# A two-layer mLSTM/retention trunk: longer waits between the steps of the gate chain, and a second buffer for head outputs

## The chip, the cores and the metric

The kernel runs on one core of one Trainium2 chip. The metric is the device time of one execution in microseconds (us); less is better. Five engines of the core take part. TensorE (PE) does matrix products and has a second sequence of weight loads (PEld) beside it, VectorE (DVE) and ScalarE (ACT) do elementwise work, GpSimd (POOL) does elementwise work and issues some DMAs, and SyncE (SP) issues most DMAs. Each engine runs its own list of instructions in a fixed order and waits at an instruction until the semaphores that it needs have been raised.

## The reference

The input is x with 1024 positions of 1024 features; there are two layers and a final RMSNorm. Each layer computes

```
h = RMSNorm(x) * (1 + scale) + shift
p = h @ W_in                                   # one wide projection
y_m = mLSTM, 4 heads of 256                    # q, k (after a short causal convolution), v, i, f, o, z
y_r = retention, 4 heads of 256                # q, k (after rotary), v, z
x = x + gate * (concat(y_m, y_r) @ W_out)
```

The mLSTM heads have two scalar gates for each position. The input gate i enters as exp(i), the forget gate f as a log-sigmoid, and both are summed along the positions under a running maximum:

```
b     = cumsum(log_sigmoid(f));  a = b + m
g     = b[l] - b[s] + i[s]                     # s <= l
m_row = max(a, max_s g)
h     = (exp(g - m_row) . (q k^T)) v / max(|den|, exp(-m_row))
```

A head's output is then normalised over its 256 features, with a LayerNorm or a GroupNorm, before it is multiplied by its gate path.

## The kernel before, in words

**Numbers.** Every operand of a large product is kept as a pair of a high and a low part, and a product of such pairs takes three matmuls (`mm3`, L177 to L179). A high part comes from an ACT cast (L404) and a low part from a subtraction on DVE or POOL (L409).

**Products.** The projection W_in is done by a scheme with 7 products instead of 8 for each block. It needs sums of the normalised input, the forms U1 to U4, which `build_forms` makes on DVE (L634 to L655). The jobs of the plan are named after what they project. A v job makes the values of two heads with 24 matmuls of 256 columns a product, about 2.9 us; the z, q, k and a jobs have 12 matmuls of 512 columns a product. The products of a job are called a11, S1, S2, a12, S3, S4 and a22. They gather in PSUM banks (px, pz) which other engines empty before the next product can write them. L775 is the ACT copy of such a bank for the q, k and z jobs, L778 and L785 are their DVE sums, L825, L826, L832 and L835 are the copy and the sums of the v jobs, and L843 is the Tanh of a z job. L832, the sum with S3, is the one after which the bank of S3 is free for a22.

**Order.** The order of PE is the order of the program, written by hand. For the other engines a scheduler orders the instructions by a simulated time line, except those marked `late` (and those of a `Later()` object, line L144 in the profile), which keep the order of the program. Side work is written as generators which are launched beside the products: after each product `tick()` runs those that are due, and `yield n` makes one wait n products.

**Gate chain.** `gate_chain` is such a generator, launched once in each layer after the two small products for the gate columns. It has 4 heads by 8 tiles of 128 positions, hence 32 rows of 128. Its steps are: ACT moves the two gate rows out of PSUM (L512); a DMA stores them (L515) and another loads them back as 32 rows (L531); ACT takes Abs, Exp and Ln (L533 to L535); DVE makes the log-sigmoid and two running sums; PE carries the sums over the tiles (L547); DVE adds the carry and makes a running maximum; PE turns the maxima of the tiles into one row (L556); DVE takes their running maximum; PE turns them back (L561); DVE adds, and a DMA stores the maxima (L567); PE transposes four arrays (L571), a DMA loads the maxima for all partitions (L575), and ACT makes three tables of exponentials (L580, L585, L596). The DVE steps go through `Later()`, so they keep their place in the program. The 32-row arrays lie in the two buffers of the pool tag "q", which the attention of the heads uses later.

**Around it.** In layer 0 the chain runs beside two more gate projections, the rotary tables (`rotary_tables`, also through `Later()`) and the v job of heads 4 and 5, then come the v job of heads 6 and 7 and the jobs z4, q4 and k4. In layer 1 it runs beside the two gate projections and the v job of heads 4 and 5, and z4 follows directly. The mLSTM heads, 0 to 3, come after the four retention heads in each layer.

**Head outputs.** `attention` is a generator for each head, and its step `values` gathers the output of a pair of tiles in a buffer: "nd" (516 columns, one buffer) for mLSTM heads, "n" (512 columns, one buffer) for retention heads. ACT writes it (L1134 for the inter-chunk part or L1148 in the first step of an mLSTM head, L1150 for retention), for mLSTM DVE adds the product (L1155), then DVE takes the statistics (L1163, L1164), ACT normalises in place (L1185), and a DVE transpose (L1192) into "zt" frees the buffer. `load_rotary` (L971) takes four 512-column buffers for the sine and cosine of the rotary step; one of them is of tag "nd". It does so at the job q4 and they are used until the rotary step of k7 is done.

Of the kernel before, what the change touches and what calls it, by code (L numbers as in the profile page):

```python
# [24 lines left out]
HD = 256  # L25
# [62 lines left out]
def tile_hybrid_trunk(ctx, tc, x, xt, c, positions, w_ada, b_ada, norm_g, w_in, w_blk, w_val, conv_w, conv_b,  # L88
# [16 lines left out]
    def nm(s):  # L105
        uid[0] += 1
        return f"{s}_{uid[0]}"

    def bt(dt=F32, n=512):
        return big.tile([P, n], dt, tag="b", name=nm("b"))  # L110

    def wt(tag, n, bufs, dt=F32):
        t = wrk.tile([P, 516 if tag == "acc" else n], dt, tag=tag, bufs=bufs, name=nm(tag))
        return t[:, 0:n] if tag == "acc" else t

    def ps_a():
        return pa.tile([P, 512], F32, tag="a", name=nm("pa"))
# [386 lines left out]
    def gate_chain(l, pgs, gt):  # L504
# [5 lines left out]
        for half in range(2):  # L510
            for r in (0, 32):
                A.activation(raw[r:r + 4, half * HALF:(half + 1) * HALF], pgs[half][r:r + 4, :], AF.Identity,  # L512
                             bias=bg[r:r + 4, :])
        for i in range(2):
            Q.dma_start(gtd[l][i], raw[32 * i:32 * i + 4, :])  # L515
        one, two = (wt("q", 1024, 2) for _ in range(2))
# [9 lines left out]
        nc.vector.memset(first, 1.0)  # L526
        nc.vector.memset(first.rearrange("p (h t) -> p h t", h=4)[:, :, 0:1], 0.0)
        nc.vector.memset(exc, 0.0)
        yield 3
        for i, t in enumerate((fb, li)):  # L530
            Q.dma_start(t, gtd[l][i].rearrange("h (b t) -> (h b) t", t=P))  # L531
        yield 3
        A.activation(e, fb, AF.Abs)  # L533
        A.activation(e, e, AF.Exp, scale=-1.0)
        A.activation(e, e, AF.Ln, bias=ones[0:32, 0:1])  # L535
        yield 2
        V.scalar_tensor_tensor(fb, fb, 0.0, e, ALU.min, ALU.subtract)
        V.tensor_scalar(lfq, fb, MAG_Q, -MAG_Q, ALU.add, ALU.add)
        V.tensor_tensor(fb, fb, lfq, ALU.subtract)
# [1 line left out]
        V.tensor_tensor_scan(br, on, fb, 0.0, ALU.mult, ALU.add)  # L541
        V.tensor_scalar(liq, li, MAG_Q, -MAG_Q, ALU.add, ALU.add)
        V.tensor_tensor(lir, li, liq, ALU.subtract)
        yield 3
        pc = ps_a()
        for i, b in enumerate((bq, br)):
            PE.matmul(pc[0:32, i:i + 1], lower, b[:, P - 1:P], start=True, stop=True)  # L547
# [3 lines left out]
        V.tensor_tensor(u, liq, bq, ALU.subtract)  # L551
        V.tensor_tensor_scan(mx, on, u, 0.0, ALU.mult, ALU.max)
        V.tensor_tensor(v, lir, br, ALU.subtract)
        yield 3
        pm = ps_a()
        PE.transpose(pm[0:1, 0:32], mx[:, P - 1:P], ident[0:32, 0:32])  # L556
        V.tensor_tensor_scan(inc[0:1], first[0:1], pm[0:1, 0:32], 0.0, ALU.mult, ALU.max)
        V.tensor_tensor(exc[0:1, 1:32], inc[0:1, 0:31], first[0:1, 1:32], ALU.mult)
        yield 3
        pb = ps_a()  # L560
        PE.matmul(pb[0:32, 0:1], exc[0:1, :], ones[0:1, 0:1], start=True, stop=True)  # L561
        V.tensor_copy(carry[:, 2:3], pb[0:32, 0:1])
# [408 lines left out]
    def load_rotary(rot):  # L971
        for which in range(2):
            for i in range(2):
                t = wt("dm", 512, 2) if which == 0 else wt("nd", 516, 1) if i == 0 else bt()
                Q.dma_start(t[:, 0:HALF], rdr[which][i])
                A.activation(t[:, 0:HALF], t[:, 0:HALF], AF.Sin, scale=2.0 * math.pi)
                rot[which].append(t[:, 0:HALF])
# [7 lines left out]
    def attention(l, hg, gt):  # L985
        h, ml = hg % 4, hg < 4
        W = HD + 2 if ml else HD
        sds = [None] * NCH
        nrm = [None] * NCH
        st = {"state": None, "cf": None}  # L990
# [115 lines left out]
        def values(j, tts):  # L1106
            state = st["state"]
            sH, sL = sds[j]
            if tts[0] == 0:
                st["nd"] = wt("nd", 516, 1).rearrange("p (a b) -> p a b", a=2) if ml else None  # L1110
                nrm[j] = st["nd"][:, :, 0:HD] if ml else wt("n", 512, 1).rearrange("p (a b) -> p a b", a=2)
            nd3 = st["nd"]
            ahead = {}
            if j == 0:
# [92 lines left out]
        def run(what):  # L1207
            op, a = what[0], [int(x) for x in what[1:]]
            j = a[0]
            if op in "qk":  # L1210
                load_qk(op, j)
            elif op in "QK":
                split_qk(op.lower(), j)
            elif op == "v":
                load_v(j)
            elif op == "t":
                kt_load(j)
            elif op == "s":
                kt_split(j)
            elif op == "d":  # L1220
                dm_load(j)
            elif op == "m":
                dm_make(j)
            elif op == "S":
                begin(scores(j))
            elif op == "V":
                values(j, tuple(a[1:]))
            elif op == "U":
                begin(update(tuple(a)))
# [240 lines left out]
    for l in range(DEPTH):  # L1470
# [23 lines left out]
        if l == 0:  # L1494
# [10 lines left out]
            for step in script.split():  # L1505
# [50 lines left out]
                elif what == "G":  # L1556
                    n = arg[0]
                    finish_gsh(0, 2 * n, 2, pad[:, 4 * n:4 * n + 2], pad[:, 4 * n + 2:4 * n + 4])
                elif what == "W":
                    i, p = arg  # L1560
                    wsp[i, p] = high(rw[i][p], q3[:, p * 512:(p + 1) * 512] if i == 2 else None)
                else:
                    i, p = arg
# [25 lines left out]
        launch(build_forms(hT, F))  # L1589
        run_units(gate_units(wg, hT, pgs))  # L1590
        launch(gate_chain(l, pgs, gt), 1)
        if l == 0:
            launch(rotary_tables(), 7)
# [26 lines left out]
        def job_product(what, arg):  # L1620
            h = arg[0]
            if what == "v":
                return vpair_product(l, F, arg)
            if what == "z":
                return pair_product(F, z_done(gdr[l][h]))
            if what == "a":
                return pair_product(F, zo_done(gdr[l][h][arg[1]]))
            which = int(what == "k")
            if h == 4 and not which:
                load_rotary(rot)  # L1630
            if h > 3:
                return pair_product(F, rot_done(l, h, which, *rot), True)
            return pair_product(F, conv_done(l, h, which), conv=True)
# [21 lines left out]
        if l == DEPTH - 1:  # L1655
# [4 lines left out]
            for cc in range(2):  # L1660
                t = bt()
# [59 lines left out]
```

## Time and profile before

| what | us |
|---|---|
| median of 3 runs | 2235.43 |
| the runs | 2228.78, 2235.43, 2241.55 |
| the execution that was profiled | 2231.53 |
| its span, from the first to the last instruction | 2229.8 |
| mean granted TensorE clock | 0.991 |
| PE busy | 2133.3 (96%) |
| DVE busy | 1779.0 (80%) |
| ACT busy | 1144.5 (51%) |
| POOL busy | 942.2 (42%) |

In the views that follow, a row of the time line gives the start and the duration in us, the engine, the line, the operation, the result and its operands, the shape, and in brackets how long the engine stood idle ahead of it and whom it waited for. A row of the waits gives the engine and the tile that waited, who ended the wait, and the total, the number and the longest. A row of the windows gives a stretch, its length, and the busy time (and number of instructions) of each engine listed, then the granted TensorE clock as a share of full speed, the busy share of the DMA engines and GB/s.

### The profile page before, as it was taken

Reading aid. Unit: us, or ns where it says so; the run is one execution under the profiler, and the core shown is the slowest. Engines: PE = TensorE matmul, PEld = TensorE weight load, DVE = VectorE, ACT = ScalarE, POOL = GpSimd, SP = SyncE. Lnnn points to the kernel's source line nnn. Section 1 sums busy time; section 2 is a strip of 40 time slices with the busy share of each in tenths; the row PEclk is TensorE's granted clock in tenths of the full one; section 3 lists DMA queues with packets and bytes.
Section 4 is the critical chain, followed back from the end, with each engine's and each line's share of the span. In section 5 each row is a group of like instructions: output and inputs, shape, how many; then the busy total and the mean of one; then the engine's idle time right before and its main releaser. Section 6 shows DMA issues by size and latency. Waiting matters only on the chain.

```text
span 2229.8 us, 35055 instructions
## 1 busy us (share of the span) xinstructions
PE 2133.3 (96%) x11489; PEld 1818.7 (82%) x11489; DVE 1779.0 (80%) x3139; ACT 1144.5 (51%) x2151; POOL 942.2 (42%) x820
## 2 busy tenths in 40 slices
PE   6889999999999999999998999999999899999998
PEld 5688789888988878888777888888987887888887
DVE  6898888999989999874639687788787888978563
ACT  7535345445556656653544434454556555555342
POOL 1433344444454444424466344444434444442313
PEclk9999999999999999999999999999999999999999
DMA  8267678787786667686632866877867677677874
GB/s 290 58 179 214 198 219 258 212 250 210 215 237 184 196 177 208 190 270 221 208 107 68 247 191 189 230 201 221 224 182 194 187 202 194 176 199 247 224 249 119
DMA packets 452836, 448.44 MB, mean 201 GB/s; under 512 B 191314, under 2 KB 310042, under 8 KB 452652
## 3 DMA queue, kind: packets, MB, share of 16 engines
q1 hardware_dynamic: 432924, 410.27, 59.3%
q0 software_dynamic: 19584, 35.66, 10.5%
q8 instruction: 90, 1.47, 0.3%
q14 instruction: 94, 0.77, 0.1%
q10 hardware_dynamic: 144, 0.26, 0.0%
HBM read 322.76 MB, written 123.31 MB: 200 GB/s over the span
## 4 chain that ended last, share of the span: by engine, by line
PE 44%; DVE 27%; DMA 14%; issue 7%; ACT 3%; POOL 2%; SPq 2%; DVEq 0%; POOLq 0%; ACTq 0%
PE px L177 5%; PE px L178 5%; PE px L179 5%; PE pz L178 4%; PE pz L179 4%; PE pz L177 4%; PE pa L177 3%; PE pa L179 3%; PE pa L178 3%; DVE acc L889 3%; DVE R L409 3%; DMA acc<-kfr 2%; DMA R<-in_w_blk_dram 2%; DVE R L713 2%; DMA R<-in_w_val_dram 2%
## 5 line engine op out<-in xcount | busy, mean ns | idle before, releaser
L404 ACT CAST wH<-R 128x512 fp32r<-128x512 f32 x616 | 378.0, 617 | 468.6 <-PE px L178 133.4
L409 POOL TENSOR_TENSOR R<-R,wH 128x512 fp32r<-128x512 f32 x276 | 391.4, 1425 | 483.5 <-ACT wH L404 317.0
L177 PE MATMUL px<-b,wH 128*128 128x512 f32 x912 | 360.7, 395 | 6.4 <-ACT acc L775 5.8
L179 PE MATMUL px<-b,R 128*128 128x512 f32 x912 | 362.1, 397 | 0.0
L178 PE MATMUL px<-b,wH 128*128 128x512 f32 x912 | 360.8, 396 | 0.0
L409 DVE TENSOR_TENSOR R<-R,wH 128x512 fp32r<-128x512 f32 x340 | 261.9, 774 | 97.7 <-ACT wH L404 87.7
L178 PE MATMUL pz<-b,wH 128*128 128x512 f32 x704 | 279.3, 397 | 1.4 <-DVE b L1266 1.4
L179 PE MATMUL pz<-b,R 128*128 128x512 f32 x704 | 280.0, 398 | 0.0
L177 PE MATMUL pz<-b,wH 128*128 128x512 f32 x704 | 279.2, 397 | 0.0
L177 PEld LDWEIGHTS px<-b,wH 128*128 128x128 f32 x912 | 172.2, 189 | 45.4 <-ACT acc L775 7.6
L179 PEld LDWEIGHTS px<-b,R 128*128 128x128 f32 x912 | 171.6, 188 | 40.3
L178 PEld LDWEIGHTS px<-b,wH 128*128 128x128 f32 x912 | 171.9, 188 | 38.6
L177 PE MATMUL px<-wH,b 128*128 128x256 f32 (+1 forms) x576 | 176.9, 307 | 15.9 <-ACT acc L825 5.8
L178 PE MATMUL px<-R,b 128*128 128x256 f32 (+1 forms) x576 | 173.8, 302 | 7.8 <-DVE R L409 7.8
L179 PE MATMUL px<-wH,b 128*128 128x256 f32 (+1 forms) x576 | 174.4, 303 | 0.0
L709 POOL DMA_DIRECT2D R<-in_w_blk_dram x104 | 93.1, 895 | 172.9 <-DMA R<-in_w_blk_dram 61.3
L178 PEld LDWEIGHTS pz<-b,wH 128*128 128x128 f32 x704 | 133.2, 189 | 32.0 <-DVE b L1266 2.3
L179 PEld LDWEIGHTS pz<-b,R 128*128 128x128 f32 x704 | 132.8, 189 | 31.3
L177 PEld LDWEIGHTS pz<-b,wH 128*128 128x128 f32 x704 | 133.2, 189 | 28.5 <-issue 0.2
L877 POOL TENSOR_TENSOR kc<-acc,kc 128x512 fp32r<-128x512 f32 x64 | 88.0, 1375 | 114.2 <-ACT kc L876 109.0
L177 PE MATMUL pz<-wH,b 128*128 128x256 f32 (+1 forms) x448 | 134.1, 299 | 0.3 <-DVE acc L785 0.3
L179 PE MATMUL pz<-wH,b 128*128 128x256 f32 (+1 forms) x448 | 133.8, 299 | 0.0
(345 smaller groups left out, 5282.3 us busy)
## 6 DMA issues: line engine op xcount, KB each, us to landing
R<-in_w_blk_dram SPq DMA_DIRECT2D x276, 256.0 KB
vdr<-acc SPq DMA_DIRECT2D x128, 256.0 KB
ring<-vdr SPq DMA_DIRECT2D x64, 512.0 KB
R<-in_w_out_dram SPq DMA_DIRECT2D x128, 256.0 KB
R<-in_w_blk_dram POOLq DMA_DIRECT2D x104, 256.0 KB, 4.6
R<-in_w_val_dram SPq DMA_DIRECT2D x80, 256.0 KB
gdr<-acc SPq DMA_DIRECT2D x64, 256.0 KB
acc<-in_w_ada_dram SPq DMA_DIRECT2D x64, 256.0 KB
```

What stands on the lines that cost most here:

```text
L177: PE.matmul(o, lt[0], rt[0], start=start, stop=False, skip_group_check=more)
L178: PE.matmul(o, lt[0], rt[1], start=False, stop=False, skip_group_check=more)
L179: PE.matmul(o, lt[1], rt[0], start=False, stop=stop, skip_group_check=more)
L404: A.copy(h, r)
L409: eng.tensor_tensor(lo, r, f(h), ALU.subtract)
L709: G.dma_start(raw[n], src, accum_op=ALU.add)
L713: V.tensor_tensor(raw[n], raw[one], raw[two], ALU.add)
L877: eng.tensor_tensor(dst[1], src, f(dst[0]), ALU.subtract)
L889: V.scalar_tensor_tensor(acc[:, e:], pt[:, o + e - d:o + HALF - d], wcol, acc[:, e:], ALU.mult, ALU.add)
```

## The change

The waits of `gate_chain` get longer. There is a new wait of 2 products ahead of the store of the gate rows. The waits that follow go from 3 to 4 (ahead of the load), 3 to 4 (ahead of Abs), 2 to 3 (ahead of the DVE scans), 3 to 6 (ahead of L547), 3 to 5 (ahead of L556) and 3 to 5 (ahead of L561); the two waits of 2 behind it stay. So the chain's last step is issued 12 products later. The head outputs of both kinds take the tag "nd", which now has two buffers of 516 columns; "n" is gone. Lines from L515 on have a number greater by one in the kernel of after.

```diff
@@ gate_chain
+        yield 2
         for i in range(2):
             Q.dma_start(gtd[l][i], raw[32 * i:32 * i + 4, :])
...
-        yield 3
+        yield 4
         for i, t in enumerate((fb, li)):
             Q.dma_start(t, gtd[l][i].rearrange("h (b t) -> (h b) t", t=P))
-        yield 3
+        yield 4
         A.activation(e, fb, AF.Abs)
...
-        yield 2
+        yield 3
         V.scalar_tensor_tensor(fb, fb, 0.0, e, ALU.min, ALU.subtract)
...
-        yield 3
+        yield 6
         pc = ps_a()
...
-        yield 3
+        yield 5
         pm = ps_a()
...
-        yield 3
+        yield 5
         pb = ps_a()
@@ load_rotary
-                t = wt("dm", 512, 2) if which == 0 else wt("nd", 516, 1) if i == 0 else bt()
+                t = wt("dm", 512, 2) if which == 0 else wt("nd", 516, 2) if i == 0 else bt()
@@ values
-                st["nd"] = wt("nd", 516, 1).rearrange("p (a b) -> p a b", a=2) if ml else None
-                nrm[j] = st["nd"][:, :, 0:HD] if ml else wt("n", 512, 1).rearrange("p (a b) -> p a b", a=2)
+                st["nd"] = wt("nd", 516, 2).rearrange("p (a b) -> p a b", a=2) if ml else None
+                nrm[j] = st["nd"][:, :, 0:HD] if ml else wt("nd", 516, 2)[:, 0:512].rearrange("p (a b) -> p a b", a=2)
```

Three places show how the instructions move. Rows that stand together are neighbours in the list of one engine; a name's number only tells buffers apart.

The first is the list of PE in layer 1, in the v job of heads 4 and 5, where S1 (pz) ends and S3 (px) begins. Before the change the two matmuls of L547 stand between them:

```order
L178 MATMUL pz_13946<-R_13818,b_13530 128x256
L179 MATMUL pz_13946<-wH_13816,b_13531 128x256
L177 MATMUL pz_13946<-wH_13816,b_13584 128x256
L178 MATMUL pz_13946<-R_13818,b_13584 128x256
L179 MATMUL pz_13946<-wH_13816,b_13585 128x256
L547 MATMUL pa_13973<-q_13547 32x1 x2
L177 MATMUL px_13725<-wH_13907,b_13441 128x256
L178 MATMUL px_13725<-R_13909,b_13441 128x256
```

After the change S3 follows S1 directly, and the same two matmuls (now L548) stand 8 products later, behind S1 of z4:

```order
L178 MATMUL pz_14229<-b_13575,wH_14124 128x512
L179 MATMUL pz_14229<-b_13574,R_14159 128x512
L548 MATMUL pa_14244<-q_13598 32x1 x2
L177 MATMUL px_14205<-b_13432,wH_14161 128x512
L178 MATMUL px_14205<-b_13433,wH_14161 128x512
```

Counted in rows of PE, L547 moves from 509 to 701 in layer 0 and from 5771 to 5939 in layer 1, L556 from 582 to 822 and from 5844 to 6000, L561 from 655 to 943 and from 5917 to 6063, and L571 from 752 to 1016 and from 5966 to 6112. No other row of PE changes its place against its neighbours.

The second place is the list of DVE in layer 1, ahead of the two L832 sums that empty the banks of S3. Before the change the chain's steps (L144, on q) lie ahead of them:

```order
L144 TENSOR_TENSOR q_13547<-q_13547 32x128
L144 SCALAR_TENSOR_TENSOR q_13547<-ones,q_13547 32x128 x2
L144 TENSOR_SCALAR q_13548<-q_13548 32x128
L144 TENSOR_TENSOR q_13547<-q_13548 32x128
L144 COPY q_13548<-pa_13973 32x2
L144 TENSOR_SCALAR q_13547<-q_13547,q_13548 32x128 x2
L144 TENSOR_TENSOR q_13548<-q_13548,q_13547 32x128
L144 SCALAR_TENSOR_TENSOR q_13548<-ones,q_13548 32x128
L144 TENSOR_TENSOR q_13548<-q_13547 32x128
L310 SCALAR_TENSOR_TENSOR acc_13712<-acc_13903,cact,acc_13712 128x512
L409 TENSOR_TENSOR R_14058<-R_13624,wH_14056 128x512
L832 TENSOR_TENSOR acc_13940<-px_13725,acc_13940 128x512
```

After the change the forms (L656, L635) and three other rows are what is left ahead of the sums (now L833), and the first step of the chain comes behind them:

```order
L656 SCALAR_TENSOR_TENSOR acc_13845<-acc_13843,acc_13845 128x512
L635 TENSOR_TENSOR acc_13885<-b_12960,b_12961 128x512
L656 SCALAR_TENSOR_TENSOR acc_13885<-acc_13883,acc_13885 128x512
L310 SCALAR_TENSOR_TENSOR acc_13710<-acc_13806,cact,acc_13710 128x512
L310 SCALAR_TENSOR_TENSOR acc_13710<-acc_13893,cact,acc_13710 128x512
L409 TENSOR_TENSOR R_14049<-R_13622,wH_14047 128x512
L833 TENSOR_TENSOR acc_13930<-px_13723,acc_13930 128x512
L833 TENSOR_TENSOR acc_13964<-px_13765,acc_13964 128x512
L144 SCALAR_TENSOR_TENSOR q_13598<-q_13598 32x128
```

The third place is the list of ACT in layer 0, ahead of the L775 copy (now L776) in the job q4. Before the change five loads of a function table stand there, for L843 (the Tanh of z4) and L976 (the sine of the rotary step) by turns:

```order
L843 ACT_TABLE_LOAD
L843 ACTIVATE acc_2601<-pz_2586 128x512
L404 CAST wH_2674<-R_2504 128x512
L976 ACT_TABLE_LOAD
L976 ACTIVATE b_2668<-b_2668 128x512
L843 ACT_TABLE_LOAD
L843 ACTIVATE acc_2631<-acc_2574 128x512
L976 ACT_TABLE_LOAD
L976 ACTIVATE dm_2662<-dm_2662 128x512
L404 CAST wH_2697<-R_2611 128x512
L843 ACT_TABLE_LOAD
L843 ACTIVATE acc_2653<-acc_2547 128x512
```

After the change the exponentials of the chain lie ahead, and three loads are left between the first Tanh and the copy:

```order
L597 ACTIVATE wd_2541<-wd_2541 128x64
L404 CAST wH_2634<-R_2556 128x512
L844 ACTIVATE acc_2601<-pz_2586 128x512
L404 CAST wH_2674<-R_2481 128x512
L844 ACTIVATE acc_2631<-acc_2574 128x512
L404 CAST wH_2697<-R_2611 128x512
L977 ACT_TABLE_LOAD
L977 ACTIVATE b_2668<-b_2668 128x512
L844 ACT_TABLE_LOAD
L844 ACTIVATE acc_2653<-acc_2524 128x512
L977 ACT_TABLE_LOAD
L977 ACTIVATE dm_2662<-dm_2662 128x512
```

Of the head outputs, on DVE of layer 0 the transpose of one buffer (L1193, nd_9712) now stands behind the statistics of the next (L1164, nd_9853), where before it stood ahead of them; many of the adds of L1155 and of the ACT writes of L1134 stand a few rows earlier than before.

## The prediction

> **What bounds the kernel now.** I read the page first, then the waits of PE, then the time line and the windows at the places where the change moves something. The page says who matters:
>
> ```profile
> PE 2133.3 (96%) x11489; PEld 1818.7 (82%) x11489; DVE 1779.0 (80%) x3139; ACT 1144.5 (51%) x2151; POOL 942.2 (42%) x820
> ```
>
> PE is busy for 2133.3 of 2229.8 us, so 96.5 us is the most that any order of the other engines could give back, apart from PE's own pace. The question is how much of it stands at the chain. The waits of PE on the tiles that the change touches:
>
> ```profile
> PE pa L547 <- DVE q L144: 10.7, 2, 8.1
> PE pa L556 <- DVE q L144: 3.0, 1, 3.0
> PE pa L177 <- ACT n L1150: 0.2, 1, 0.2
> ```
>
> The gate chain costs PE 13.7 us in three waits; the head outputs cost it 0.2 us. So the two parts of the change are very unequal before anything is moved. On the time line the three waits of the chain, and two others that are needed below, are these:
>
> ```profile
> 129.18 0.53 PE L547 MATMUL pa<-q 32*32 32x1 f32 x4 [2.62 <-DVE q L144]
> 137.38 0.39 PE L177 MATMUL px<-wH,b 128*128 128x256 f32 x1 [0.25 <-DVE acc L832]
> 143.49 0.19 PE L556 MATMUL pa<-ident,q 32*1 32x32 f32 x1 [2.96 <-DVE q L144]
> 224.43 0.50 PE L177 MATMUL px<-b,wH 128*128 128x512 f32 x1 [2.71 <-ACT acc L775]
> 1229.56 0.58 PE L547 MATMUL pa<-q 32*32 32x1 f32 x4 [8.07 <-DVE q L144]
> ```
>
> In each wait PE stands at a tiny matmul of the chain because DVE hasn't reached the chain's step ahead of it. The windows give PE's pace around them, and the last row shown is a stretch of the same matmuls without a wait:
>
> ```profile
> 126.56:143.49 16.93, 11.01 (x78) 0.90 0.47 164
> 143.49:154.04 10.55, 10.55 (x75) 0.84 0.89 238
> 1221.50:1243.24 21.74, 13.63 (x102) 0.84 0.69 201
> 160.00:177.00 17.00, 17.00 (x144) 1.00 0.74 187
> ```
>
> The full pace is 17.00/144 = 0.118 us a matmul. In layer 0, 153 matmuls took 16.93 + 10.55 = 27.48 us where the pace gives 18.05; in layer 1, 102 took 21.74 where it gives 12.04. So **9.4 us are at stake in layer 0 and 9.7 us in layer 1**. It is more than the waits because the granted clock falls behind them:
>
> ```profile
> 130.50:133.90 3.40, 3.40 (x19) 0.50 0.34 116
> 144.10:147.50 3.40, 3.40 (x19) 0.50 0.87 160
> 1226.20:1233.00 6.80, 3.39 (x17) 0.50 1.00 292
> 224.43:228.00 3.57, 3.57 (x15) 1.00 0.86 263
> ```
>
> Each wait at the chain is followed by some 3.4 us at a clock of 0.50: 19 matmuls in 3.40 us instead of 19 x 0.118 = 2.24, so 1.2 us lost each time. The wait of 2.71 us at 224.43 was followed by none.
>
> **Who is late when the chain isn't.** The stages as a whole (busy times of PE, PEld, DVE, ACT and POOL in this order):
>
> ```profile
> 116.00:213.00 97.00, 89.94 (x652) 85.47 (x651) 90.09 (x193) 37.84 (x68) 36.20 (x27) 0.96 0.70 195
> 640.00:990.00 350.00, 336.88 (x1681) 281.52 (x1680) 316.27 (x603) 212.47 (x411) 150.42 (x146) 0.99 0.72 207
> 1178.00:1234.00 56.00, 45.53 (x294) 39.40 (x293) 55.52 (x63) 27.88 (x47) 36.77 (x24) 0.94 0.34 91
> 1690.00:2060.00 370.00, 355.07 (x1921) 304.41 (x1920) 308.30 (x599) 214.17 (x413) 154.31 (x150) 0.99 0.70 198
> ```
>
> The first and the third row are the chain's stages. DVE works 90.09 of 97 us and 55.52 of 56. It isn't the length of the chain that makes PE wait but DVE's queue: the chain's steps lie behind forms and rotary work. A longer distance in products doesn't take work from DVE, it only lets PE go on with products, until PE needs something else that lies in the same queue.
>
> **Term A, the chain in layer 0.** L547 moves by 192 rows and L556 by 240, so both waits (2.62, 2.96) go from where they are. What is late next is the L832 sum that empties S3's bank for a22; it was late already, by the 0.25 us at 137.38. Of the chain, what lies ahead of that sum on DVE starts and ends here (the second row is the rotary step behind it):
>
> ```profile
> 124.92 1.37 DVE L144 SCALAR_TENSOR_TENSOR q<-q 32x128 f32<-32x128 f32 x1
> 129.81 0.28 DVE L144 CAST acc<-acc 128x256 f32<-128x256 int32 x1
> ```
>
> That is 129.81 - 124.92 = 4.89 us for the chain's steps up to the first scans. They go behind the sum, and I put 1 us of rotary work in their place, since `Later()` steps follow the program: the sum and a22 come 3.9 us earlier, at about 133.5 instead of 137.38. PE would be there by 137.38 - 2.62 - 0.53 - 1.2 = 133.0, so a wait of 0.5 to 1.4 us appears and at most 3.9 is won up to there. Of the second wait and its slow clock (2.96 + 1.2) I count only about 0.6, since the postponed steps still have to be done by a DVE with 6.9 idle us in 97. **A = 4.5 us**, with 2 (only part of the first wait) and 9.4 (all that is at stake) as bounds.
>
> **Term B, the chain in layer 1.** On DVE, the last run of chain steps ahead of L832, and the sum:
>
> ```profile
> 1225.63 0.27 DVE L144 SCALAR_TENSOR_TENSOR q<-q 32x128 f32<-32x128 f32 x1
> 1228.90 0.27 DVE L144 TENSOR_TENSOR q<-q 32x128 f32<-32x128 f32 x1
> 1233.62 0.73 DVE L310 SCALAR_TENSOR_TENSOR acc<-acc,cact,acc 128x512 f32<-128x512 f32 x1
> 1234.89 0.67 DVE L832 TENSOR_TENSOR acc<-px,acc 128x512 f32<-128x512 f32 x1
> ```
>
> From 1228.90 to 1233.62 there are 4.72 us of chain, and some 0.3 more in the two steps from 1225.63 on, which lie between forms. Behind the change all of it comes after both sums: the first sum starts at about 1234.89 - 5.0 = 1229.9 and a22 at about 1230.7. Before, S3 had two parts of 24 matmuls, begun at 1229.56 + 0.58 with the slow clock until 1233: 1233.0 - 1230.1 = 2.9 us for 14 of them, and 34 x 0.118 = 4.0 for the rest, hence a22 at 1237.1. That is 6.4 us earlier. But PE, without the wait of 8.07, has S3 done at 1221.5 + 48 x 0.118 = 1227.2 and waits 3.5 us for the sum. **So the wait of 8.07 turns into one of about 3.5 at a22.** The slow clock behind it may cost 1.2 again, of which 0.9 stood in the 6.4 already: **B = 5.5 us**, between 3.5 (the forms that a22 needs are late too) and 9.7.
>
> The Trainium skill, "TensorE: Matmul & The Clock Gate", Part 1: The HAM clock gate, says that the half clock comes after at least one idle window of about 3.4 us, with windows that run freely. The rows differ: waits of 2.62 and 2.96 us were enough, one of 2.71 wasn't. By the page the new wait in layer 1 would bring the half clock and those of layer 0 none, and the sum would be some 1 us larger.
>
> **Term C, the loads of ACT's tables.** The wait at 224.43 is for an L775 copy which stands behind this on ACT:
>
> ```profile
> 212.70 1.28 ACT L843 ACT_TABLE_LOAD   x1 [4.52 <-DVE pz L778]
> 217.06 1.28 ACT L843 ACT_TABLE_LOAD   x1
> 219.00 1.28 ACT L976 ACT_TABLE_LOAD   x1
> 221.46 1.28 ACT L843 ACT_TABLE_LOAD   x1
> 223.79 0.58 ACT L775 COPY acc<-px 128x512 f32<-128x512 f32 x1
> ```
>
> Of five loads there (the fifth, of L976, lies between the first two shown), three are left between the first Tanh and the copy, so the copy can come 2 x 1.28 = 2.56 us earlier. The exponentials that moved ahead of them meet an ACT that stood idle for 4.52 us. I take **C = 1.5 us** (0 if the copy then waits for its own product, 2.7 if all of the wait goes).
>
> **Term D, the second buffer.** The waits on the transpose that frees an output buffer, and those of the mLSTM add:
>
> ```profile
> ACT n L1150 <- DVE zt L1192: 11.3, 8, 2.9
> ACT nd L1134 <- DVE zt L1192: 2.5, 4, 0.8
> ACT nd L1148 <- DVE zt L1192: 2.1, 2, 1.2
> DVE nd L1155 <- ACT nd L1134: 5.0, 4, 2.2
> ```
>
> ACT waits 15.9 us in all on that transpose, but it is busy for only 51%, and PE felt 0.2 us of it. For retention heads, where most of it lies, one of the two buffers is the rotary table's until k7, so nothing frees. For mLSTM heads the buffer lets L1134 write earlier, and PE idles 350 - 336.88 = 13.1 and 370 - 355.07 = 14.9 us in those stages, each wait of another cause. **D = 0**, from -6 to +6: a few of those 28 us could go, or as many come, as the scheduler's order changes in the whole stage.
>
> **What the later steps may wait for.** The distances behind L561 stay (2 and 2 products), and q and k of the attention need the buffers "q" only some ten products after the chain's end in its new place, so I put nothing for either. In layer 1 the three tables now arrive among the products of z4 and q4. If that cover were gone, the mLSTM heads, first to read them, still come after four retention heads.
>
> **The sum.** 4.5 + 5.5 + 1.5 + 0 = 11.5 us. The profiled execution took 2231.5, so 2220.0 on its own scale; the median of the runs stands 3.9 us above it, which makes 2223.9. I forecast between the two, **2222 us**. With the bounds, the forecast's own range is 2207 (all 19.1 us of A and B, and the 6 of D: 2231.5 - 25.1) to 2229 (A and B at their lower ends: 2231.5 - 5.5 + 2).
>
> **Rivals.**
>
> *The next wait takes nearly all.* DVE has 0.5 us of slack in 56 and 6.9 in 97. If a form or the low part of a22 is late as well, 2 and 2 us are left: about 2230. For it speaks the wait of 0.25 us on L832, already the next late thing; against it that the moved steps really leave DVE's queue ahead of that sum (4.89 and 5.0 us).
>
> *The half clock stays.* If the new waits are followed by as much slow clock as the old ones, A and B lose 1.2 x 3 = 3.6: about 2226. The rows of 2.62 and 2.96 speak for it, that of 2.71 against it.
>
> *Slower: the adds of the head outputs come too early.* With two buffers, the scheduler puts many L1134 writes and L1155 adds a few rows earlier. An engine takes its list in order, so an L1155 that stands ahead of its product holds up all of DVE, and behind it the scores and state sums for which PE waits. The price of one is in the row of L1155: 5.0/4 = 1.25 us. There are 48 of them; if every one waited and half reached PE, it would be 48 x 1.25 / 2 = 30 us, and the time about 2250 after the gain. It decides from 11.5/24 = 0.48 us an add on. Against it speaks that DVE is idle there for 33.7 of 350 us and could absorb a part.
>
> *The change doesn't do what it says.* The chain's steps on DVE slip behind as much as its matmuls, the same waits stand at new places, and the table takes the second buffer: 2231 to 2235, say 2233.
>
> **Chances.** Forecast 0.47, next wait 0.17, half clock 0.11, slower 0.18, nothing done 0.07. About 0.5% (11 us, so below 2224.3) is what a measurement of this kernel can tell from no change. Of the forecast's chance 0.42 lies below that line and of the half clock's 0.04; the rest of those, the next wait and nothing done lie within 0.5%. That is 0.46 faster, 0.36 the same, 0.18 slower. The range leaves out the longest gains (0.07) and the upper part of the slower case (0.12): **2208 to 2243**; 2207 to 2229 is the likeliest case's own.
>
> **What would show it.** In the changed profile L548 and L557 have no wait of over 1 us; a wait for the L833 sum stands at a22, near 1 us in layer 0 and 3 to 4 in layer 1; the wait ahead of 224 is shorter than 1.2 us; ACT's waits on the transpose fall while PE's busy time in the mLSTM stages stays within 6 us. The prediction is wrong if L548 waits at its new place, if the wait at a22 is over 6 us in layer 1, or if DVE's waits at L1156 rise beyond 12 us.

## The result and the profile after

| | us |
|---|---|
| before, median of 15 runs | 2235.36 (2226.33 to 2243.82) |
| after, median of 15 runs | 2227.21 (2218.94 to 2233.52) |
| ratio, 95% interval | 0.9966 [0.9954, 0.9979] |
| the profiled execution of after, span | 2224.6, clock 0.987 |

The ratio is a gain of 7.6 us (4.7 to 10.3), where 11.5 us was the sum and 13.4 the distance from the median to the forecast of 2222. The sign and the places were right, and the two large terms were too large. The busy times say little, as PE's work is the same:

```profile
PE 2137.0 (96%) x11489; PEld 1820.5 (82%) x11489; DVE 1776.2 (80%) x3139; ACT 1146.9 (52%) x2151; POOL 945.0 (42%) x820
```

The waits of PE after (who waited for whom; total, times, longest) have no row for L548 or L557 any more. In place of their 13.7 us stands the sum that empties S3's bank:

```profile
PE px L177 <- DVE acc L833: 13.2, 4, 5.2
PE pa L1122 <- POOL sL L1080: 9.1, 8, 3.3
PE pa L177 <- ACT nd L1151: 2.1, 1, 2.1
PE pa L177 <- ACT nd L1135: 1.5, 2, 1.2
```

On PE's time line after, the two new waits at a22 and the shorter one in q4 are these rows:

```profile
136.74 0.55 PE L177 MATMUL px<-wH,b 128*128 128x256 f32 x1 [5.25 <-DVE acc L833]
220.08 0.50 PE L177 MATMUL px<-b,wH 128*128 128x512 f32 x1 [1.03 <-ACT acc L776]
1230.83 0.55 PE L177 MATMUL px<-wH,b 128*128 128x256 f32 x1 [5.07 <-DVE acc L833]
```

The same matmuls began at 137.38, 224.43 and 1237.17 before. PE's windows after show that the slow clock came with the new waits too:

```profile
134.90:141.70 6.80, 4.96 (x23) 0.50 0.52 150
1230.60:1234.00 3.40, 3.17 (x15) 0.50 0.88 276
```

In the first of them 23 matmuls took 4.96 us instead of 23 x 0.118 = 2.71, in the second 15 took 3.17 instead of 1.77: 2.2 and 1.4 us lost.

**How a stage's gain is read below.** PE's list is the same in all kernels but for the chain's few matmuls (and, in the three named s4, the order within the v jobs, in ada_later that of adaLN products from 1272 us of before on). So the same matmul can be found in two traces, and the difference of its start times says how far ahead PE is there. Taken between two points it is the gain of that stage alone, whatever came earlier. The layer-0 stage is taken from 118 to 235 us of before, which holds A and C, and the layer-1 stage from 1207 to 1290, which holds B.

| kernel | ratio, 95% interval | layer-0 stage, us | layer-1 stage, us |
|---|---|---|---|
| after | 0.9966 [0.9954, 0.9979] | -3.5 | -4.0 |
| after_again | 0.9962 [0.9946, 0.9978] | -3.5 | -2.4 |
| chain_only | 0.9976 [0.9964, 0.9989] | -3.5 | -2.3 |
| chain_l0 | 0.9976 [0.9962, 0.9990] | -3.6 | -0.2 |
| chain_l1 | 0.9984 [0.9971, 0.9996] | 0.0 | -3.1 |
| buffer_only | 0.9994 [0.9976, 1.0012] | -1.5 | +0.2 |
| back_only | 0.9983 [0.9969, 0.9997] | -1.6 | +0.2 |
| front_only | 0.9977 [0.9963, 0.9992] | -3.1 | -3.6 |
| ada_later | 0.9969 [0.9952, 0.9987] | -1.5 | -3.8 |
| rot_later | 1.0006 [0.9994, 1.0018] | -5.8 | -4.4 |
| s4_after | 1.0022 [1.0008, 1.0037] | +0.9 | +0.4 |
| s4_before | 1.0022 [1.0009, 1.0035] | +2.0 | +0.1 |
| s4_free | 1.0003 [0.9986, 1.0020] | 0.0 | -4.4 |

A minus sign means that PE gained on before. Each stage figure comes from one execution. Stages that a kernel doesn't touch show the grain: 0.0 and -0.2 in chain_l1 and chain_l0, but -1.5 in layer 0 of buffer_only. In the same way ada_later has the list of after in the layer-0 stage, but gave 1.5 us there, and rot_later has it in the layer-1 stage.

### The profile page after: what moved, and what is told of

The parts are those of the page before. It is cut to its first block, busy times and chain, and to the rows that moved or that the text cites. A ratio compares the mean times of both kernels' runs of the same rounds, so it can differ in the third digit from the quotient of the medians.

```text
span 2224.6 us, 35050 instructions
## 1 busy us (share of the span) xinstructions
PE 2137.0 (96%) x11489; PEld 1820.5 (82%) x11489; DVE 1776.2 (80%) x3139; ACT 1146.9 (52%) x2151; POOL 945.0 (42%) x820
## 4 chain that ended last, share of the span: by engine, by line
PE 54%; DVE 23%; DMA 11%; issue 6%; ACT 3%; POOL 2%; SPq 1%; DVEq 0%; POOLq 0%; ACTq 0%
PE px L177 7%; PE px L178 7%; PE px L179 7%; PE pz L179 6%; PE pz L178 6%; PE pz L177 6%; PE pa L179 4%; PE pa L177 4%; PE pa L178 4%; DVE acc L890 3%; DMA acc<-kfr 3%; DVE R L409 2%; DVE acc L635 2%; DMA R<-in_w_val_dram 2%; PE pa L1131 1%
## 5 line engine op out<-in xcount | busy, mean ns | idle before, releaser
L409 POOL TENSOR_TENSOR R<-R,wH 128x512 fp32r<-128x512 f32 x276 | 395.0, 1437 | 483.2 <-ACT wH L404 314.9
L409 DVE TENSOR_TENSOR R<-R,wH 128x512 fp32r<-128x512 f32 x340 | 262.8, 776 | 92.1 <-ACT wH L404 88.9
L177 PEld LDWEIGHTS px<-wH,b 128*128 128x128 f32 x576 | 114.5, 199 | 30.5 <-issue 11.9
L177 PE MATMUL pz<-wH,b 128*128 128x256 f32 (+1 forms) x448 | 134.3, 300 | 0.4 <-DVE acc L786 0.2
```

The costliest lines, as they stand in the source:

```text
L177: PE.matmul(o, lt[0], rt[0], start=start, stop=False, skip_group_check=more)
L409: eng.tensor_tensor(lo, r, f(h), ALU.subtract)
```

## The experiments

**The two parts apart.** chain_only has the new waits with the old buffers:

```diff
-                t = ... wt("nd", 516, 2) if i == 0 else bt()
+                t = ... wt("nd", 516, 1) if i == 0 else bt()
-                nrm[j] = ... else wt("nd", 516, 2)[:, 0:512].rearrange(...)
+                nrm[j] = ... else wt("n", 512, 1).rearrange(...)
```

> Only the longer waits of the gate chain; "nd" has one buffer and "n" is there as before. As forecast (the second buffer is worth nothing): the same gain as the whole change, 7.6 us (ratio 0.9966) within 3 us. Rival, the second buffer costs what the head stages gave back in the profile after (3.4 us): 11 us faster than before, ratio 0.995. Rival, the gain comes from the second buffer: no gain, ratio 1.000. In the trace under the first two: no wait at L548 and L557, waits of about 5 us for the L833 sums in both layers.

buffer_only has the new buffers with the old waits, the opposite edit.

> Only the shared tag "nd" with two buffers; the chain's waits are those of before. As forecast: no change within 2 us, with ACT's waits on the transpose into zt clearly under the 15.9 us of before. Rival, it costs: 3 to 4 us slower, with new waits of PE in the head stages on ACT's writes of nd. Rival, it is the gain: 7.6 us faster.

The chain alone gave 5.4 us (2.5 to 8.0), the buffers 1.3 us (from 2.7 slower to 5.4 faster). So most of the gain is the chain's, and that the buffers alone make the whole of 7.6, or cost 3 us, lies outside the interval. The trace says more of the buffers than the time can. The waits of PE in the head stages of chain_only (one buffer) and of buffer_only (two):

```profile
PE pa L177 <- DVE cf L1100: 8.4, 4, 2.7
...
PE pa L179 <- DVE b L930: 4.0, 7, 0.9
PE pa L177 <- ACT n L1151: 3.6, 1, 3.6
PE pa L1122 <- POOL sL L1080: 3.6, 5, 1.3
```

```profile
PE pa L1121 <- POOL sL L1079: 8.7, 6, 3.4
PE pa L179 <- DVE b L929: 4.2, 5, 1.4
PE pa L1121 <- ACT sH L1078: 3.3, 2, 2.7
PE pa L177 <- ACT nd L1134: 1.5, 2, 1.2
```

The wait for the state sum (cf) is there in all five kernels with one buffer, before among them (6.1 to 8.4 us), and in none of the nine with two. Where the order of the products is kept, the wait for the low part of the scores (sL, at L1121 or L1122) is 3.1 to 6.6 us in the former and 8.6 to 11.7 in the latter, and 1.5 us for the write of nd come new. With the other head waits (sH, the scores' sums, the scaled keys, nd and n) PE waited 20.0 to 25.4 us with one buffer, 23.4 in the mean of before and three others (chain_only, chain_l0, chain_l1), and 19.1 to 23.8 with two, 20.9 in the mean of six (after, after_again, buffer_only, back_only, front_only, ada_later). The buffer takes one wait away and lets the next appear. The 2.5 us between the two means aren't a gain that is shown. The wait of L1130 (L1131) for the low part of the state (cL), which isn't in these sums, goes the other way, from 1.4 to 2.3 us in the mean. And by the start times of the same matmuls the stretches from 335 to 990 and from 1290 to 2060 took 1.8 us longer than in before with two buffers (mean of the six, from 4.7 less to 9.7 more) and 1.5 us longer with one (mean of the four, from 2.6 less to 5.2 more). Neither the time nor the traces tell the buffer's worth from nothing.

**The two layers apart.** In chain_l1 each new wait holds in layer 1 alone, in chain_l0 in layer 0 alone:

```diff
-        yield 6
+        yield (3, 6)[l]
```

> The longer waits of the chain in layer 1 alone, one buffer each as before. As the profile after reads: 4 to 5 us faster than before, PE 10 us ahead when the first S3 begins and 5.5 after the wait for the L833 sum. If the gain of layer 1 is lost again later (a later stage waits for a transfer at a fixed time): under 2 us. If layer 0 does all: 0.

> The longer waits of the chain in layer 0 alone, one buffer each as before. As the profile after reads: 3 to 4 us from the chain's stage and 1 us from the shorter wait for the L776 copy in q4, so 4 to 5 us faster; if the head stages of layer 0, which in the profile after gave back 3.9 us until 482 us, do so because of the chain's new place, under 1 us. Added to the gain of layer 1 alone it should make that of both.

Layer 1 alone gave 3.6 us (0.9 to 6.5), layer 0 alone 5.4 (2.2 to 8.5). The stage figures, -3.1 and -3.6, stand in the one layer and not in the other, and make 6.7 together, beside 5.4 for both by time. The sum of the two measured gains, 9.0, is more than that of both, but the intervals are too wide to make anything of it.

chain_l1 served for another question. Its list of instructions is that of before, engine by engine, up to layer 1. Still PE lost 2.9 us from 335 to 600 against the profile of before; at 990 it was only 0.5 us behind. The profile after lost 4.2 us in the same stretch, which looked like a price of the change. chain_l1 shows that about 3 us there can be nothing but one execution against another. It doesn't show that all of it is: with two buffers the six kernels lost 4.2 to 7.3 us there, with one the four lost 0.0, 0.1, 2.9 and 4.5, so a price of the buffer in this stretch stays possible. From 335 to 990 it is 1.4 to 5.1 and 0.0 to 3.4 us.

**Which of the new waits pay.** back_only takes the four waits ahead of the scans back and keeps 6, 5 and 5; front_only keeps those four and goes back to 3, 3 and 3.

```diff
-        yield 2
         for i in range(2):
             Q.dma_start(gtd[l][i], raw[32 * i:32 * i + 4, :])
...
-        yield 4
+        yield 3
...
-        yield 4
+        yield 3
...
-        yield 3
+        yield 2
```

> The kernel of after with the four waits ahead of the scans as before (no extra 2, then 3, 3, 2) and only the three behind them longer (6, 5, 5), two buffers kept. Theory now: what pays is that the chain's DVE steps fall behind the L833 sums. Here the first seven steps stay ahead of them and only the second group goes behind: in layer 1 the first sum at about 1233.5 instead of 1230.0, a wait of 8 us for it, and 2 us of gain there; in layer 0 as in after; together 3 us less gain than after, about 4.5 us below before (ratio 0.998). Rival, the longer distance between a step and its matmul is what pays: the full 7.6 us (0.9966).

```diff
-        yield 6
+        yield 3
...
-        yield 5
+        yield 3
...
-        yield 5
+        yield 3
```

> The kernel of after with the four waits ahead of the scans as in after and the three behind them as before (3, 3, 3), two buffers kept. Theory now: all of the chain's DVE steps lie behind the L833 sums as in after, PE reaches L548 only after a22, so no wait over 1 us at L548 and the gain of after, 7 us (ratio 0.997). Rival, the distance pays: waits of 2 to 8 us come back at L548 and L557 and under 3 us of gain is left.

In layer 1 the two differ by 3.9 us. In layer 0 they gave 1.6 and 3.1, which is within what one list gave there (1.5 to 3.6). The row of a22 in back_only, and then in front_only:

```profile
1236.38 0.55 PE L177 MATMUL px<-wH,b 128*128 128x256 f32 x1 [7.14 <-DVE acc L833]
```

```profile
1233.79 0.55 PE L177 MATMUL px<-wH,b 128*128 128x256 f32 x1 [5.06 <-DVE acc L833]
```

In back_only the matmul L548 no longer waits either, but the chain's first seven steps on DVE still lie ahead of the sum, so PE waits 7.14 us instead of 8.07 and the stage gives +0.2. In front_only L548 stands only one product behind a22 and has no wait over 1 us. So the distance between a step and its matmul doesn't pay; that the chain's DVE steps fall behind the sum does. By time front_only (5.1 us, 1.8 to 8.3) isn't told from after, nor from back_only (3.8, 0.7 to 6.9).

**Is it DVE's queue that makes a22 late?** ada_later starts the adaLN rows (L308, L310) of layer 1 ten products later, so that they are gone from ahead of the sum.

```diff
-        launch(adaptive(l, gcol, gb), 2 if l else 30)
+        launch(adaptive(l, gcol, gb), 12 if l else 30)
```

> The kernel of after with the adaLN rows of layer 1 (L308, L310) begun 12 instead of 2 products behind the gate columns, so that they fall behind the two L833 sums on DVE. Theory: the wait of 5.07 us at a22 in layer 1 is DVE's queue; without 4.7 us of L310 rows and their wait for a DMA the sum comes at 1225.5, and the wait falls to 0 to 2 us, since the low parts of the forms from POOL are done at 1227.7. That is 3 to 4 us less than after, 11 us below before (ratio 0.995). Rival, something else is as late (forms, weights): the wait stays over 4 us with another releaser and the time is that of after.

The rival was right, but that PE's wait still ended with the L833 sum. DVE after (first fence) had the adaLN rows ahead of the sum; in ada_later (second fence) DVE stands idle in their place:

```profile
1224.81 1.78 DVE L310 SCALAR_TENSOR_TENSOR acc<-acc,cact,acc 128x512 f32<-128x512 f32 x1
1227.65 1.83 DVE L310 SCALAR_TENSOR_TENSOR acc<-acc,cact,acc 128x512 f32<-128x512 f32 x1 [1.07 <-DMA acc<-in_w_ada_dram]
1230.01 1.27 DVE L833 TENSOR_TENSOR acc<-px,acc 128x512 f32<-128x512 f32 x2
1231.21 0.27 DVE L144 SCALAR_TENSOR_TENSOR q<-q 32x128 f32<-32x128 f32 x1
```

```profile
1226.31 2.12 DVE L656 SCALAR_TENSOR_TENSOR acc<-acc,acc 128x512 f32<-128x512 f32 x1
1230.69 1.51 DVE L409 TENSOR_TENSOR R<-R,wH 128x512 fp32r<-128x512 f32 x1 [2.26 <-ACT wH L404]
1232.12 1.28 DVE L833 TENSOR_TENSOR acc<-px,acc 128x512 f32<-128x512 f32 x2
```

The sum lies behind an L409, which waits for a cast of ACT, and ACT's list has the cast behind the rounding of the last form U4, which L656 finishes only at 1228.4. So the wait at a22 stayed at 4.53 us. In layer 1 the forms, not only the queue, set the time; the 4.7 us that were taken from DVE ahead of the sum bought half a us of wait, and the time is that of after (0.9969).

rot_later does the same in layer 0 with the rotary steps:

```diff
-            launch(rotary_tables(), 7)
+            launch(rotary_tables(), 13)
...
                 V.tensor_tensor(dst, turn, rnd, ALU.subtract)
-                yield 1
```

> The kernel of after with the rotary tables begun 13 instead of 7 products behind (and one wait of 1 product in each of their 8 parts left out, so that they end in time), which puts all rotary steps on DVE behind the two L833 sums of layer 0. Theory: the wait of 5.25 us at a22 in layer 0 is DVE's queue; 6 to 7 us of rotary steps leave it, the sum comes before 131 and the wait falls under 2 us; some of that comes back in later waits of the same stage, as DVE's work is only postponed: 2 to 4 us less than after over the stage. Rival, DVE simply has too much to do in this stage: the wait moves on in full, PE is as late at 200 us as in after, and the time is that of after.

Here the first theory held at the place, and the rival for the whole. Two rows of PE in rot_later:

```profile
133.71 0.36 PE L177 MATMUL px<-wH,b 128*128 128x256 f32 x1 [1.89 <-DVE acc L833]
252.88 0.37 PE L322 MATMUL pa<-ones,acc 128*128 128x1 f32 x1 [6.25 <-DVE acc L310]
```

The wait at a22 fell from 5.25 to 1.89 us, and at 156 PE was 8.8 us ahead of before instead of 3.6. But the rotary steps then met the adaLN rows and the jobs z4 and q4 on DVE; at 252.88 PE waited 6.25 us for a sum of those rows, and at 335 it was 3.1 us behind before. The time was that of before.

**Covering the wait with another product.** s4_after exchanges the last two products of the v jobs, so that S4 stands between S3 and a22; s4_before does so in the kernel of before. after_again is the kernel of after once more, beside them.

```diff
-    VNAMES = ("a12", "a11", "S2", "S1", "S3", "a22", "S4")
+    VNAMES = ("a12", "a11", "S2", "S1", "S3", "S4", "a22")
```

> The kernel of after unchanged, once more, beside the next two on the same chip: 0.9966 of before within 0.0013, and a second profile that shows which of its waits repeat. If the stage account is right, the waits for the first L833 sums are again 5.0 to 5.4 us in both layers and there is none over 1 us at L548 and L557, while the head stages differ from the first profile by up to 4 us either way.

> The kernel of after with the last two products of the v jobs exchanged: S4 before a22, so that 5.7 us of products stand between S3 and the a22 that waits for the L833 sum. Theory: PE had nothing else to do in the waits of 5.25 and 5.07 us, and S4 needs only the L831 copies, done at 1225.6 and 1227.2; both waits fall under 1.5 us, up to 8 us less than after in these stages, and 3 to 8 in the time: ratio 0.993 to 0.995 to before. Rival, S4's own weights or copies are as late: the waits move to S4 and the time is that of after.

> The kernel of before with the same exchange and nothing else. Theory: the waits at L547 and L556 stand ahead of S3 or behind it and stay as they are (2.6, 3.0 and 8.1 us), so the time is that of before within 3 us, since a22 had a wait of 0.25 us only. Rival, the exchange gains by itself 5 us or more, without the chain's new place.

after_again repeated the result, 8.5 us (4.9 to 12.1), with waits of 5.01 and 5.35 us at a22 and none over 1 us at the chain. s4_before was slower by 4.9 us (2.0 to 7.8), which neither theory had. In s4_after the waits at a22 did go (PE was 9.6 us ahead at 156), and the time still became 4.9 us longer than before. One row of PE in s4_before, then PE, DVE and ACT of s4_after, in four fences:

```profile
198.00 0.79 PE L177 MATMUL px<-b,wH 128*128 128x512 f32 x1 [4.50 <-DVE acc L800]
```

```profile
193.26 0.50 PE L177 MATMUL px<-b,wH 128*128 128x512 f32 x1 [3.58 <-DVE acc L801]
1248.95 0.80 PE L177 MATMUL px<-b,wH 128*128 128x512 f32 x1 [4.94 <-DVE acc L801]
```

```profile
1248.20 0.69 DVE L801 SCALAR_TENSOR_TENSOR acc<-px,acc 128x512 fp32r<-128x512 f32 x1 [0.30 <-ACT acc L798]
```

```profile
1247.50 0.60 ACT L798 ACTIVATE acc<-px 128x512 fp32r<-128x512 f32 x1 [1.49 <-DMA vdr<-acc]
```

a22 leaves its result in the px bank, and L798 and L801 read it straight from there. Where a22 comes last, the next job's first product needs that bank at once, and L798 stands waiting for a buffer that a store must free. In the old order S4 stands between the two. In s4_before the same wait (L800 is L801 there) took 4.50 us, the granted clock was 0.50 from 197.3 to 204.1, and PE fell back by 7.5 us between 195 and 200. s4_free copies the bank first, so that PE needn't wait for the pair:

```diff
                 else:
-                    launch(store(part, 1, 0, bank["X"]))
+                    c = wt("acc", 512, NACC)
+                    A.copy(c, bank["X"])
+                    launch(store(part, 1, 0, c))
```

> The kernel with the exchanged products and the chain's place of after, and one edit more: the last product's bank is copied by ACT, and the store works from the copy, so the bank is free before the slow L798 and L801 pair has read it. Theory: the new waits of that kernel (3.58 and 4.94 us at the next a11, for L801) are the price of the exchange, and go to under 1.5 us; with the waits for L833 covered as well, up to 8 us less than the exchanged kernel, ratio to before 0.995 to 0.998. If it also comes under 0.9964 it beats after. Rival, the next thing in line (weights, forms of the next job) is as late: the waits move once more and the ratio stays at 1.002.

The two waits became those for L840, the copy; the two rows for L826 and L776 are other waits of layer 0:

```profile
162.24 0.58 PE L177 MATMUL px<-wH,b 128*128 128x256 f32 x1 [3.07 <-ACT acc L826]
191.51 0.51 PE L177 MATMUL px<-b,wH 128*128 128x512 f32 x1 [1.13 <-ACT acc L840]
209.29 0.50 PE L177 MATMUL px<-b,wH 128*128 128x512 f32 x1 [2.94 <-ACT acc L776]
1243.62 0.50 PE L177 MATMUL px<-b,wH 128*128 128x512 f32 x1 [0.78 <-ACT acc L840]
```

The theory of the bank held: 3.58 and 4.94 became 1.13 and 0.78. The layer-1 stage then gave 4.4 us, as much as the best execution with after's list there (4.4, rot_later). Layer 0 kept nothing: PE was 9.9 us ahead at 156, lost 3.6 of them between 160 and 170 at a new wait for an L826 copy (3.07, with half the clock from 162.0 to 165.5) and 4.7 between 210 and 215, at a wait for an L776 copy (2.94, with half the clock from 209.8 to 213.2). The head stages gave back the rest; the ratio of 1.0003 is short of the 0.995 to 0.998 expected. What is lost in the head stages of layer 1 here (12.4 us against after_again from 1290 to the end, by one execution of each, with single waits of 4.9 us for L892 and 4.4 for sL) has no experiment of its own and stays open. No version tried beats after.

## Why the prediction was right, and where its sizes were off

*At stake, 9.4 and 9.7 us.* The reading of the chain's waits held: the waits at L547 and L556 went to nothing wherever waits of the chain were lengthened (the front ones, those behind, or both), and stayed at 11.0 and 2.4 us in buffer_only.

*Term A, 4.5 us, with C 1.5: 6.0 in the layer-0 stage.* Measured 3.5 to 3.6 us in four executions with this list and 1.5 in the fifth, ada_later, so 3.1 in the mean. In the fifth a short wait was followed by half the clock:

```profile
182.51 0.36 PE L177 MATMUL px<-wH,b 128*128 128x256 f32 x1 [1.76 <-DVE acc L833]
183.90:187.30 3.40, 3.40 (x19) 0.50 0.77 159
```

The list of before gave 0.0, 0.0 and 1.5 (before itself, chain_l1, buffer_only), so that 2.6 lie between the means. The step that failed is the one that put the sum and a22 3.9 us earlier, with 1 us of rotary work in place of the chain's 4.89. DVE after, from the forms on:

```profile
122.04 2.38 DVE L656 SCALAR_TENSOR_TENSOR acc<-acc,acc 128x512 f32<-128x512 f32 x2
125.14 3.49 DVE L635 TENSOR_TENSOR acc<-b,b 128x512 f32<-128x512 f32 x2
131.59 1.48 DVE L144 SCALAR_TENSOR_TENSOR acc<-acc 128x256 f32<-128x256 f32 x1
134.65 0.68 DVE L409 TENSOR_TENSOR R<-R,wH 128x512 fp32r<-128x512 f32 x1
135.91 0.68 DVE L833 TENSOR_TENSOR acc<-px,acc 128x512 f32<-128x512 f32 x1
```

The sum began at 135.91 instead of 136.65: 0.74 us earlier, not 3.9. Two things filled the chain's place. The pair of form sums at 125.14 took 3.49 us, and its counterpart before took 1.27:

```profile
130.61 1.27 DVE L634 TENSOR_TENSOR acc<-b,b 128x512 f32<-128x512 f32 x2
136.65 0.68 DVE L832 TENSOR_TENSOR acc<-px,acc 128x512 f32<-128x512 f32 x1
```

It now runs beside two POOL subtractions of 3.54 us:

```profile
124.54 3.54 POOL L878 TENSOR_TENSOR b<-acc,b 128x512 fp32r<-128x512 f32 x2 [1.28 <-ACT b L877]
```

Before, the slow neighbours of POOL were three of the chain's small steps, which took 1.2 to 1.4 us each beside these rows, and the pair at 130.61 had no POOL row beside it:

```profile
124.42 3.01 POOL L877 TENSOR_TENSOR b<-acc,b 128x512 fp32r<-128x512 f32 x2
127.39 1.25 POOL L409 TENSOR_TENSOR R<-R,wH 128x512 fp32r<-128x512 f32 x1
133.48 1.29 POOL L877 TENSOR_TENSOR b<-acc,b 128x512 fp32r<-128x512 f32 x1 [4.83 <-ACT b L876]
```

So, as far as these rows show, 4.89 us was not the chain's own price but partly POOL's, and POOL's stayed. In after_again the pair took 1.28 us again, but a cast of 0.28 took 1.38 and an L803 of 0.68 took 1.78 in its place, and the sum began at 135.58. And four more rotary steps, 1.4 us, moved ahead of the sum, where I had put 1 us, and the one at 131.59 took 1.48 us instead of 0.41. PE therefore waited 5.25 us instead of 0.5 to 1.4. The other half of the step was too cautious: of the wait at L556 and its slow clock I had counted 0.6 us, and all of the 2.96 went. The two errors, in opposite directions, leave about 2 us in the first profile (3.5 less some 1.6 at the L776 copy), which is A's lower bound; that the stage still gave about half of its 6.0 us is in part luck.

*Term C, 1.5 us.* Right: the wait of 2.71 us became 1.03 and 1.42 in the two profiles of after, 1.29 in chain_l0, and stayed at 2.70 and 2.62 in buffer_only and chain_l1, where the tables come in the old order.

*Term B, 5.5 us.* Measured 2.3 to 4.4, 3.2 in the mean of the five executions with the list of after in this stage (after, after_again, chain_only, chain_l1, rot_later). The time of the sum was forecast to 0.1 us (1229.9, measured 1230.01), but partly by luck, since PE was 1.0 us ahead at 1207 already. The wait was 5.07 instead of 3.5, since PE finished S3 at 1230.83 - 5.07 = 1225.76 and not 1227.2. Two sizes were off. a22's lead was forecast as 6.4; it began 6.3 us earlier in after, but counted from 1207 that is 5.3, and 5.0 in the mean of the five. And behind a22 the prediction put the price of the slow clock at 1.2 and took only 0.9 off; the five lost 1.2 to 2.6 us between a22 and 1290, 1.8 in the mean: 1.2 and 1.3 in the two with 3.4 us at half the clock there, 2.0 to 2.6 in the three with 6.8.

*Half the distance of the medians.* From the sum of 11.5 I went 2 us further down, as I took the time halfway between the profiled execution's scale and that of the median. No row supported that step: it is medians that are compared, so 2223.9 was the time that goes with the sum. (The range's lower end is off by less: 2231.5 - 25.1 is 2206.4, not 2207.)

*The next wait takes nearly all.* This rival, with a chance of 0.17, was half true. The wait for the L833 sum became 5.25 us in layer 0, where I had looked for 0.5 to 1.4, and 5.07 in layer 1, and A was left with the 2 us that it says; B kept more than its 2.

*The half clock.* A rival with a chance of 0.11, it was largely true: 3.6 us were lost to it at the two places after (2.2 and 1.4), about as much as in the three stretches before (1.2, 1.2 and 1.4), and its time of 2226 is nearer to the measured 2227.2 than the forecast is. The Trainium skill, "TensorE: Matmul & The Clock Gate", Part 1: The HAM clock gate, says that the half clock comes after at least one idle window of about 3.4 us. The waits of 5.25 and 5.07 us agree with that, being longer; those of 2.62 and 2.96 before, which also brought it, don't fit. The length of a wait alone doesn't decide: the one of 2.71 before brought none, and the wait of 1.76 in ada_later brought it where one of 1.77 at the same matmul of after_again brought none.

*Term D, 0 us.* Not told from 0. PE's head waits changed by a mechanism that I hadn't named, the state sums on DVE, so that PE felt only 0.2 us on the buffer itself was true and not the whole; but other waits took their place. ACT's waits on the transpose, for mLSTM, went entirely. For retention 10.1 of 11.3 us stayed: they stand between 349 and 454 and at 1437, while the rotary table holds one of the buffers (its last reads are at 517 and 1542). These are ACT's and DVE's rows after:

```profile
ACT nd L1151 <- DVE zt L1193: 10.1, 5, 3.5
DVE nd L1156 <- ACT nd L1135: 3.6, 3, 1.7
```

and PE's windows in the two mLSTM stages (with PEld, DVE, ACT and POOL) are busier by 2.0 and 1.4 us than before, within the 6 us forecast:

```profile
640.00:990.00 350.00, 338.83 (x1690) 282.51 (x1689) 307.25 (x603) 213.74 (x413) 150.35 (x147) 0.99 0.74 209
1690.00:2060.00 370.00, 356.45 (x1917) 305.15 (x1916) 309.26 (x597) 216.26 (x416) 152.98 (x148) 0.99 0.71 199
```

That isn't the buffer's gain: in chain_l1, with one buffer, PE's waits in the same two stretches were 11.6 and 12.0 us, beside 11.0 and 13.4 after and 13.1 and 14.9 before.

*The slower rival.* It didn't come: the adds of L1156 waited 3.6 us for ACT after, 5.0 before.

By the means of the executions the two stages make 2.6 + 3.2 = 5.8 us (6.3 against the one profile of before), with nothing that is shown for the buffer, beside 5.4 (2.5 to 8.0) by time for the chain alone and 7.6 (4.7 to 10.3) for the whole change. The 2 us between aren't told from noise.

## What to carry to other kernels

A wait of PE at a small side step says which queue it waits in, not what the step costs. Moving the step to where PE comes later gains only up to the next instruction of the same queue that PE needs, so look for that one first and work out its new time from the whole list, other helpers' steps and POOL's work beside it included. An exchange of products that removes a wait can take away the cover of another (S4 over the release of a bank), and work that is put off returns where it is due. Before a few us of a stage are read from two profiles, compare two executions over a stretch in which the programs are the same.

## What the runs showed of the hardware

The same DVE instruction on the same shape (L634/L635, 128x512) took about 0.64 us a piece in some places (1.27 for two) and 1.74 in others (3.49 for two), the latter while POOL had subtractions running (3.54 us for two). In the profile of before 15 of 41 such sums were slow, and each had a POOL subtraction beside it for over half of its time; but so had 7 of the 26 quick ones, so that isn't enough to make one slow. A chain step on 32x128 took 0.2 to 0.4 us alone and up to 1.37 beside POOL. At the chain's place in layer 0 the slow stretch didn't move with the work: it caught the form pair in after, and a cast and an L803 in after_again. And two executions of one list of instructions differed by 2.9 us within 265 us of the span (335 to 600, before and chain_l1).
